# Merging the 16-blocks of eight triangular inverses with 32x32 products on a compact block layout

## The chip, the cores and the metric

The kernel runs on one core of a Trainium2 chip. The metric is the device time of one execution in microseconds. Five engines with an instruction queue each work side by side: TensorE (PE in the rows; its weight loads are PEld), VectorE (DVE), ScalarE (ACT), GpSimd (POOL) and SyncE (SP, which here only starts transfers). An engine takes its instructions in program order; engines wait for each other by semaphores.

## What is computed

Two decoder layers on x of 256 tokens by 1024 features: a gated-DeltaNet layer and a softmax-attention layer, each followed by a residual LayerNorm. The change touches the first layer, where the reference solves a unit lower triangular system in every chunk and head:

```
lower = jnp.where(strict, jnp.einsum('nbhid,nbhjd->nbhij', k_beta, k) * decay, 0.0)
a_mat = jnp.eye(C, dtype=jnp.float32) + lower
w = lax.linalg.triangular_solve(a_mat, k_beta * jnp.exp(gc)[..., None],
                                left_side=True, lower=True, unit_diagonal=True)
u = lax.linalg.triangular_solve(a_mat, v * beta[..., None],
                                left_side=True, lower=True, unit_diagonal=True)
```

## The kernel before

The kernel works with chunks of 128 tokens, so 2 chunks by 8 heads give 16 triangular matrices of 128x128. It inverts them in two groups of four heads, eight matrices (q = 0 to 7) in each. All large products are done as three products of rounded halves (hi times hi, hi times lo, lo times hi); the weights come in units of 128x1024 (`raw`), which ACT rounds (`hi`) and DVE subtracts (`lo`).

The order on TensorE comes out of a planner that runs while the program is built. `Pipeline` holds chains (generators) with a rank; each `yield` says on which engine the next step starts and which tiles it needs, and a step is put out when `Clock`, a model of the engines' times, says that its operands are there. Between chains TensorE gets the next projection products: for the heads' keys and queries (`ps_kq`), values (`ps_v`), gates (`ps_z`, 128x256, six products to two tokens' halves), then the output projection (`ps_y`, 128x512), then the second layer (`ps_bv`, `ps_bkq`, `ps_bz`). The order is fixed once the program is built.

One group's path, in `inverse` (lines 696 to 813):

- The matrices go to memory (`md<-ME`, on POOL's queue) and come back as 64 blocks of 16x16 (`inv<-md`). POOL inverts these by substitution, 15 steps of two small `TENSOR_TENSOR` on `inv`, then a `COPY`, and sends the inverses and their transposes to memory (`td<-inv`). SP brings them back with eight transfers (`TR<-td`) onto the diagonals of `TR`, 128x2x8x128, which POOL has cleared (`MEMSET TR`).
- `merge16` makes 32-blocks out of pairs of 16-blocks with products of full 128x128: M times T (`ps_x`), the result times the transposed inverse (`ps_y`), a masked copy into `TR` on DVE (mask `m32`), and four transposes (`ps_r`) that give the other orientation. It runs twice in a group, on four matrices each.
- `merge32` makes 64-blocks with 32x32 products (`ps_x5`, `ps_y5`; the rows call them `ps_x` and `ps_y`), and the rest of `merges` makes the 128-blocks with 64x64 products (`ps_x6`, `ps_y6`). ACT takes each intermediate out of PSUM into X.
- `solve` (line 860) then multiplies with the values (`ps_s1`, `ps_s2`, `ps_s3`; `ps_s` in the rows), and `read_out` makes the heads' outputs (`ps_o`): squares on ACT, `rs` on DVE and POOL, `og` on DVE, transposes (`ps_og`) on TensorE, and `o` on ACT and DVE, which `ps_y` reads.

The first group's outputs feed the first half of `ps_y` (48 products of 128x512) and the second group's the other 48. After these come the residual and LayerNorm of tokens 0 to 127 (`late`, `x` in the rows; `late` is read from memory into the place of `ME` once the last `ps_o` has read it), whose transposes `ps_t` open the second layer.

## Time and profile before

| | before |
|---|---|
| median of 3 runs | 309.72 us (308.55 to 311.87) |
| the profiled execution, its own time | 308.79 us |
| its span | 307.1 us |
| TensorE busy | 296.2 us, 96% |
| VectorE, ScalarE, GpSimd busy | 204.8, 166.4, 57.5 us |
| granted TensorE clock | 1.00 from 0 to 280 us, 0.94 in the rest |

The span is the time between the first and the last recorded instruction. A matmul's recorded duration goes on after the next one has begun, so what a product costs TensorE is the distance between starts, not its duration; a TensorE that is 96% busy by durations can still be slower or faster per product. A float32 product stands in the records as two, since it takes two passes over its weights.

### The profile page before, as it was taken

To read this page: it belongs to the slowest core of one execution; us is meant where nothing else is said; L and a number is where in the kernel's file an instruction comes from. 1 tells how busy PE (TensorE), PEld (TensorE's weight loads), DVE (VectorE), ACT (ScalarE), POOL (GpSimd) and SP (SyncE) were. 2 spreads that over 40 slices of the span, in tenths; PEclk is the share of its full clock that TensorE was granted. 3 is DMA by queue.
4 is the path that set the end of the run, shared out by engine and by line. 5 is a ranking of instruction groups with operands and counts; after the bars stand their busy time and mean duration, and the time that the engine had idled before them with its cause. 6 is when DMAs were issued, how large, how long until landed. Compare 5 with 4: busy or idle time off the path is not lost. (4 is left out here: it accounts for less than half of the span.)

```text
span 307.1 us, 5956 instructions
## 1 busy us (share of the span) xinstructions
PE 296.2 (96%) x2294; PEld 273.9 (89%) x2294; DVE 204.8 (67%) x440; ACT 166.4 (54%) x341; POOL 57.5 (19%) x114
## 2 busy tenths in 40 slices
PE   8999999999999999999999999999999999999990
PEld 7798988999999999989988678899999999998890
DVE  1589489999996287635475994675655555762645
ACT  3579986557566466655542514875555558461000
POOL 3002310188821886001100110000000000000101
PEclk9999999999999999999999999999999999999997
DMA  6995515565859044504069551896334447400011
GB/s 209 401 288 182 172 45 196 171 228 164 270 128 354 12 143 152 151 3 138 1 213 349 192 205 34 244 339 208 123 130 157 148 152 253 138 2 0 2 68 68
DMA packets 19307, 49.39 MB, mean 161 GB/s; under 512 B 6256, under 2 KB 7152, under 8 KB 19280
## 3 DMA queue, kind: packets, MB, share of 16 engines
q1 hardware_dynamic: 18016, 46.46, 45.4%
q0 software_dynamic: 544, 1.44, 1.8%
q10 hardware_dynamic: 720, 1.11, 1.1%
q8 instruction: 18, 0.29, 0.4%
q14 instruction: 9, 0.07, 0.1%
HBM read 46.65 MB, written 2.36 MB: 160 GB/s over the span
## 5 line engine op out<-in xcount | busy, mean ns | idle before, releaser
L217 DVE TENSOR_TENSOR lo<-raw,hi 128x1024 fp32r<-128x1024 f32 x78 | 94.9, 1226 | 13.1 <-ACT hi L217 12.9
L217 ACT CAST hi<-raw 128x1024 fp32r<-128x1024 f32 x78 | 80.2, 1048 | 16.9 <-PE ps_y L217 8.7
L217 PE MATMUL ps_y<-hi,o 128*128 128x512 f32 (+1 forms) x144 | 41.6, 371 | 0.0
L217 PE MATMUL ps_bkq<-x1h,hi 128*128 128x256 f32 x128 | 38.0, 297 | 0.0
L217 PE MATMUL ps_kq<-xh,hi 128*128 128x256 f32 x128 | 36.8, 288 | 0.0
L217 PE MATMUL ps_kq<-xh,lo 128*128 128x256 f32 x128 | 35.9, 280 | 0.5 <-DVE lo L217 0.5
L217 PE MATMUL ps_kq<-xl,hi 128*128 128x256 f32 x128 | 35.8, 279 | 0.0
L217 PE MATMUL ps_bkq<-x1l,hi 128*128 128x256 f32 x128 | 35.5, 278 | 0.0
L217 PE MATMUL ps_bkq<-x1h,lo 128*128 128x256 f32 x128 | 35.5, 277 | 0.0
L217 POOL TENSOR_TENSOR mv<-mv,nhalf 128x1 f32<-128x1 f32 x4 | 3.8, 949 | 145.9 <-DVE mv L217 145.9
L217 PEld LDWEIGHTS ps_y<-hi,o 128*128 128x128 f32 x144 | 26.1, 188 | 4.6
L217 PE MATMUL ps_y<-lo,o 128*128 128x512 f32 (+1 forms) x72 | 26.4, 367 | 0.0
L217 POOL TENSOR_TENSOR inv<-inv 64x15 f32<-64x15 f32 (+7 forms) x60 | 24.1, 401 | 4.5
L217 PEld LDWEIGHTS ps_kq<-xh,lo 128*128 128x128 f32 x128 | 24.0, 188 | 0.7 <-DVE lo L217 0.7
L217 PEld LDWEIGHTS ps_bkq<-x1h,hi 128*128 128x128 f32 x128 | 24.1, 188 | 0.2
L217 PEld LDWEIGHTS ps_bkq<-x1l,hi 128*128 128x128 f32 x128 | 24.1, 188 | 0.2
L217 PEld LDWEIGHTS ps_kq<-xl,hi 128*128 128x128 f32 x128 | 24.2, 189 | 0.0
L217 PEld LDWEIGHTS ps_kq<-xh,hi 128*128 128x128 f32 x128 | 24.2, 189 | 0.0
L217 DVE SCALAR_TENSOR_TENSOR cv<-ps_kq,cst_sb,cv 128x255 f32<-128x255 f32 (+2 forms) x48 | 21.3, 470 | 4.1 <-ACT cv L217 4.1
L217 PEld LDWEIGHTS ps_bkq<-x1h,lo 128*128 128x128 f32 x128 | 24.0, 188 | 0.0
L217 PE MATMUL ps_v<-xh,hi 128*128 128x256 f32 x64 | 18.6, 291 | 0.0
L217 PE MATMUL ps_bz<-x1h,hi 128*128 128x256 f32 x64 | 18.3, 285 | 0.0
(172 smaller groups left out, 686.7 us busy)
## 6 DMA issues: line engine op xcount, KB each, us to landing
raw<-in_wp_dram SPq DMA_DIRECT2D x78, 512.0 KB, 4.0
md<-ME POOLq DMA_DIRECT2D x8, 128.0 KB, 2.8
late<-in_x_dram SPq DMA_DIRECT2D x1, 1024.0 KB, 7.0
zraw<-in_w_dram ACTq DMA_DIRECT2D x3, 272.0 KB, 5.8
x_sb<-in_xt_dram SPq DMA_DIRECT2D x3, 256.0 KB, 5.6
ag<-in_a_ln_g_dram SPq DMA_DIRECT2D x1, 512.0 KB, 7.7
ab<-in_a_ln_b_dram SPq DMA_DIRECT2D x1, 512.0 KB, 8.4
bg<-in_b_ln_g_dram SPq DMA_DIRECT2D x1, 512.0 KB, 5.8
```

What stands on the lines that cost most here:

```text
L217: r = f(*args, **kw)
```

## The change

The 16-blocks of a group are brought back to a compact layout: of `TR`'s 2048 columns the last part now holds `TC`, 128x2x8x32, where each of the four groups of 32 partitions has its own 32x32 block with two 16-blocks on the diagonal. The eight matrices are handled at once, not four and four.

- The step from 16 to 32 is four 32x32 products per matrix for M times T (`ps_x`, 32 in a group), a masked copy of 128x256 into `XI`, an identity that is set up once per group at the kernel's start, and then eight 32x32 products per matrix (`ps_y`, 64 in a group), which give both orientations: no transposes. ACT copies both into `TC`.
- POOL copies the blocks from `TC` onto the diagonals of `RR` and `T64` (six copies of 32x256 in a group), since the later steps read them there.
- `ps_x5` and `ps_y5` run on `TC` for eight matrices (16 and 24 products), and `ps_x6` and `ps_y6` for eight (8 and 8, as before 4 and 4 twice), with the two halves' roles exchanged.
- The group's steps are one chain that goes on into `solve`. `Clock` charges 15 ns for a product over at most 32 partitions.

```
+                if reads[0].ap[0][1] <= 32:
+                    cost = 15
...
+    XI = [cst.tile([P, 8, 32], F32, name=f"XI{g}") for g in range(2)]
+    for b in blocks:
+        for g in range(2):
+            nc.gpsimd.tensor_copy(XI[g][b], ident[b, b].unsqueeze(1).to_broadcast([32, 8, 32]))
...
-        TR[grp] = act.tile([P, 2, 8, P], F32, tag=f"kq{grp}", name=f"TR{grp}")
-        nc.gpsimd.memset(TR[grp], 0.0)
+        T = act.tile([P, 2048], F32, tag=f"kq{grp}", name=f"TR{grp}")
+        nc.gpsimd.memset(T, 0.0)
+        RR = TR[grp] = T[:, 0:1024].rearrange("p (q c) -> p q c", q=8)
+        TC = T[:, 1024:1536].rearrange("p (w q c) -> p w q c", w=2, q=8)
+        T64 = T[0:64, 1536:2048].rearrange("p (q c) -> p q c", q=8)
...
-        def merge16(q0):
...
-            ps = bank([4, P], "ps_x")
-            for q in range(4):
-                nc.tensor.matmul(ps[:, q, :], ms(q0 + q), TT[:, q0 + q, :], start=True, stop=True)
...
-            for q in range(4):
-                nc.tensor.matmul(ps[:, q, :], RR[:, q0 + q, :], X[:, q, :], start=True, stop=True)
...
-            for q in range(4):
-                nc.tensor.transpose(ps[:, q, :], TT[:, q0 + q, :], ident)
...
-        for q0 in (0, 4):
-            pipe.add(merges(q0), R_INV)
-        pipe.add(solve(grp), R_SOLVE)
+        yield "t", [TC, free("b")]
+        ps = bank([8, 32], "ps_x")
+        for q in range(8):
+            for b in blocks:
+                nc.tensor.matmul(ps[b, q, :], ms(q)[b, b], TC[b, 0, q, :], start=True, stop=True)
+        yield "v", [ps, XI[grp]]
+        nc.vector.copy_predicated(XI[grp], m32.to_broadcast([P, 8, 32]), ps)
+        end(ps)
+        yield "t", [XI[grp], free("b")]
+        ps = bank([2, 8, 32], "ps_y")
+        for q in range(8):
+            for b in blocks:
+                nc.tensor.matmul(ps[b, 0, q, :], TC[b, 1, q, :], XI[grp][b, q, :], start=True, stop=True)
+            for b in blocks:
+                nc.tensor.matmul(ps[b, 1, q, :], XI[grp][b, q, :], TC[b, 1, q, :], start=True, stop=True)
+        yield "a", [ps]
+        nc.scalar.copy(TC, ps)
+        end(ps)
+        yield "t", [TC, free("b")]
+        for b in blocks:
+            nc.gpsimd.tensor_copy(RR[b, :, b], TC[b, 1])
+            if b.start < 64:
+                nc.gpsimd.tensor_copy(T64[b, :, b], TC[b, 0])
...
+        n_inv[grp] = 1
+        yield from solve(grp)
```

The built programs show what the planner makes of it. On POOL, behind the clearing of the second group's tiles (`inv_1311` before, `inv_1323` now), stood its inversion, with the first group's `rs` in its middle:

```order
L217 MEMSET inv_1311 64x16
L217 TENSOR_TENSOR inv_1311<-inv_1311 64x15 x2
...
L217 TENSOR_TENSOR inv_1311<-inv_1311 64x6x10 x2
L217 TENSOR_TENSOR rs<-rs,nhalf 128x4
L217 TENSOR_TENSOR inv_1311<-inv_1311 64x5x11 x2
...
L217 COPY inv_1311<-inv_1311 64x256
L217 DMA td<-inv_1311 64x2x256
```

Now it is:

```order
L219 MEMSET inv_1323 64x16
L219 COPY TR_836<-TR_836 32x8x32 x6
L219 TENSOR_TENSOR inv_1323<-inv_1323 64x15 x2
...
L219 COPY inv_1323<-inv_1323 64x256
L219 TENSOR_TENSOR rs<-rs,nhalf 128x4
L219 DMA td<-inv_1323 64x2x256
```

The first group's six copies stand ahead of the second group's inversion, and `rs` stands between the inversion and its transfer.

On TensorE, where the second group's merges begin (`TR_1314` before, `TR_1326` now), stood:

```order
L217 MATMUL ps_x<-TR_1314,ME 128x128 x8
L217 MATMUL ps_vt<-ident,cv 128x128 x2
L217 MATMUL ps_y<-X,TR_1314 128x128 x8
L217 MATMUL ps_z<-hi_1248,xh 128x256
L217 MATMUL ps_z<-lo_1249,xh 128x256
L217 MATMUL ps_z<-hi_1248,xl 128x256
L217 MATMUL ps_r<-ident,TR_1314 128x128 x4
```

Now it is:

```order
L219 MATMUL ps_x<-TR_1326,ME 32x32 x32
L219 MATMUL ps_og<-ident,og 128x128 x4
L219 MATMUL ps_z<-hi_1298,xh 128x256
...
L219 MATMUL ps_z<-hi_1517,xl 128x256
L219 MATMUL ps_y<-XI_146,TR_1326 32x32 x4
L219 MATMUL ps_y<-TR_1326,XI_146 32x32 x4
```

What moved: between the two groups' first merge products there are now 102 `ps_z` products where there were 57, and the second group's later steps stand between `ps_y` products of the output projection. Before, the second group's first `ps_og` stood ahead of all 96 `ps_y`; now 48 stand ahead of it, and only eight `ps_o` lie between it and the first `ps_y` that reads its result.

At the end of the output projection the second group's last `ps_og` stood 51 `ps_y` products ahead of the first that reads its result. Now these are its rows, `hi_2097` with `lo_2098` being the last weights for tokens 0 to 127, and `hi_1792` the first for tokens 128 to 255:

```order
L219 MATMUL ps_y<-hi_1907,o_2189 128x512
L219 MATMUL ps_og<-ident,og 128x128 x4
L219 MATMUL ps_y<-hi_2097,o_2189 128x512
L219 MATMUL ps_y<-lo_2098,o_2189 128x512
L219 MATMUL ps_y<-hi_2097,o_2189 128x512 x2
L219 MATMUL ps_y<-lo_2098,o_2189 128x512
L219 MATMUL ps_y<-hi_2097,o_2189 128x512
L219 MATMUL ps_y<-hi_1792,o_2189 128x512
```

What moved: six products now stand between the last `ps_og` and the first that reads it.

## Rows read from the trace of the kernel before

**Rows 1.** The page: each engine's busy us, share of the span, instructions.
```profile
PE 296.2 (96%) x2294; PEld 273.9 (89%) x2294; DVE 204.8 (67%) x440; ACT 166.4 (54%) x341; POOL 57.5 (19%) x114
```

**Rows 2.** Waits of TensorE: us in total, times, longest.
```profile
PE ps_t L217 <- DVE x L217: 0.5, 1, 0.5
```

**Rows 3.** Timeline of TensorE: start us, us, what; ends of the first group's merges.
```profile
92.57 1.99 PE L217 MATMUL ps_x<-TR,ME 128*128 128x128 f32 x16
...
104.37 1.05 PE L217 MATMUL ps_s<-W,TR 128*128 128x128 f32 x8
```

**Rows 4.** The same, ends of the second group's merges.
```profile
127.60 1.95 PE L217 MATMUL ps_x<-TR,ME 128*128 128x128 f32 x16
...
139.09 1.05 PE L217 MATMUL ps_s<-W,TR 128*128 128x128 f32 x8
```

**Rows 5.** The same, one 32x32 step between ps_z products.
```profile
99.20 0.28 PE L217 MATMUL ps_z<-hi,xl 128*128 128x256 f32 x1
99.41 0.21 PE L217 MATMUL ps_y<-X,TR 32*32 32x32 f32 x1
99.42 0.22 PE L217 MATMUL ps_y<-TR,X 32*32 32x32 f32 x2
99.47 0.19 PE L217 MATMUL ps_y<-X,TR 32*32 32x32 f32 x1
...
99.66 0.19 PE L217 MATMUL ps_y<-X,TR 32*32 32x32 f32 x1
...
100.01 0.28 PE L217 MATMUL ps_z<-lo,xh 128*128 128x256 f32 x1
```

**Rows 6.** The same, one 64x64 step between ps_z products.
```profile
103.11 0.28 PE L217 MATMUL ps_z<-hi,xl 128*128 128x256 f32 x1
103.31 0.67 PE L217 MATMUL ps_y<-TR,X 64*64 64x64 f32 x8
...
104.14 0.28 PE L217 MATMUL ps_z<-lo,xh 128*128 128x256 f32 x1
```

**Rows 7.** The same, the second group's end and the output projection.
```profile
146.90 0.60 PE L217 MATMUL ps_og<-ident,og 128*128 128x128 f32 x4
...
147.70 1.95 PE L217 MATMUL ps_o<-Z,ME 128*128 128x128 f32 x16
149.40 0.48 PE L217 MATMUL ps_y<-hi,o 128*128 128x512 f32 x1
...
170.99 0.40 PE L217 MATMUL ps_y<-hi,o 128*128 128x512 f32 x1
```

**Rows 8.** Timeline of GpSimd: the last step ahead of the second group's inversion.
```profile
102.90 0.50 POOL L217 MEMSET inv<- 64x256 f32 x2
```

**Rows 9.** GpSimd's instructions by shape: count, busy us, mean ns, idle before.
```profile
L217 POOL TENSOR_TENSOR inv<-inv 64x64 f32<-64x64 f32 x4 | 5.1, 1284 | 0.3
...
L217 POOL COPY inv<-inv 64x256 f32<-64x256 f32 x2 | 1.2, 618 | 0.1
L217 POOL MEMSET inv<- 64x256 f32 x2 | 0.6, 316 | 0.0
```

**Rows 10.** Timeline of SyncE: the second group's last two transfers, the residual's.
```profile
124.48 0.94 SPq L217 DMA_DIRECT2D TR<-td  x2
...
159.55 1.04 SPq L217 DMA_DIRECT2D late<-in_x_dram  x1
```

**Rows 11.** Transfers: count, KB each, median us from issue to landing.
```profile
late<-in_x_dram SPq DMA_DIRECT2D x1, 1024.0 KB, 7.0
...
TR<-td SPq DMA_DIRECT2D x16, 16.0 KB, 2.2
```

**Rows 12.** Timeline of VectorE: long subtractions, an output half, the LayerNorm's start.
```profile
108.03 2.54 DVE L217 TENSOR_TENSOR lo<-raw,hi 128x1024 fp32r<-128x1024 f32 x2
...
148.32 0.75 DVE L217 SCALAR_TENSOR_TENSOR o<-ps_og,nnw,o 128x512 fp32r<-128x512 f32 x1 [1.71 <-ACT o L217]
...
166.63 0.69 DVE L217 SCALAR_TENSOR_TENSOR late<-late,ps_y 128x512 f32<-128x512 f32 x1 [3.20 <-PE ps_y L217]
```

## The prediction

> **What bounds the kernel now.** I read the page first: TensorE is busy for 296.2 of 307.1 us, VectorE for two thirds of it, ScalarE for half [rows 1]. Then the waits of TensorE: there are five kinds with 3.1 us in all, and the only one behind the kernel's first third is 0.5 us on a LayerNorm's output [rows 2]. So in the stretch of the change TensorE has a product to start at almost any moment, and whatever is taken out of its queue shortens the kernel, unless something else then comes too late. I priced the products by the distance of starts in the timeline, since the recorded durations overlap. From the first `ps_y` product of 512 columns at 149.40 to the one at 170.99 [rows 7] there are 92 distances and four transposes, so (21.59 - 0.45)/92 = 0.23 us each; a `ps_z` or `ps_v` product has 256 columns, which I price at half, 0.115 us; and a transpose at 0.11, since from the `ps_og` at 146.90 to the `ps_o` at 147.70 lie four of them and, by the program's order, three `ps_z`: (0.80 - 0.35)/4.

> **What the merges cost now.** The first group's merges stretch from 92.57 to the first `ps_s` at 104.37, 11.80 us [rows 3]. By the program's order 18 `ps_z` products (2.07 us) and four transposes of values (0.44) lie in between, which leaves 9.3 us. The second group's take 11.49 us [rows 4], with 21 `ps_z` and two transposes in them: 8.9 us. Together 18.2 us of TensorE.

> **What they cost after.** One 32x32 step can be priced alone [rows 5]: twelve products, 24 records, between `ps_z` products that start at 99.20 and 100.01. The records come in eight rounds, each with one record of each of three tiles of the array. The rounds from 99.47 to 99.66 are 0.032 us apart (six distances), so eight take 0.26. Of the 0.81 us two `ps_z` take 0.23; the remaining 0.32 is what it costs to go into small tiles and out again. In the new first step four tiles have a product in each round. The three tiles of rows 5 start within 0.01 us of each other and the round waits for its tile to be free again, so I take a fourth as free and price 0.032 us per round too; the other end, each record in its turn, is a rival below.

> Of this the trace shows three tiles that write one PSUM bank side by side: `ps_y5` is one bank, and its records start 0.01 us apart while each lasts 0.2 [rows 5]. [...]

> A group then has: `ps_x`, 16 rounds, 0.51 + 0.32 = 0.83; `ps_y`, 32 rounds, 1.34; `ps_x5` and `ps_y5`, 16 rounds, 0.83 each. A 64x64 step of eight records takes 1.03 - 0.23 = 0.80 with its transitions, and its records are (0.67 - 0.22)/7 = 0.06 us apart (0.22 being one's duration) [rows 6]; sixteen take 1.28, twice. That is 6.4 us a group, 12.8 in all: **5.4 us less** TensorE time, 2.9 of it in the first group.

> **Where TensorE may now wait.** (1) The second group's blocks. Before, the last of SyncE's eight transfers starts at about 124.97 (the second of two in 0.94 us from 124.48) [rows 10] and lands 2.2 us later [rows 11], at 127.2; TensorE begins at 127.60 [rows 4], so 0.4 us of slack. After, two things move. TensorE arrives 2.9 us earlier for the first group's saving, but the planner has put 45 more `ps_z` (5.2 us) and two fewer short transposes (0.2) ahead: 127.6 - 2.9 + 5.2 - 0.2 = 129.7. The blocks come later, since POOL's queue is one line: the first group's six copies stand behind the clearing that ends at 103.40 and ahead of the inversion [rows 8]. `rs` stood inside that stretch and stays in it, so it adds nothing. A copy of 32x256 is not in the trace; by elements per partition it lies between a MEMSET of 256 (0.316 us) and a transposing COPY of 256 (0.618) [rows 9]. I take 0.5, nearer to the copy: 3.0 us. Also, a POOL step that meets a long `lo` subtraction on VectorE stretches: the 64x64 steps have a mean of 1.28 us although a MEMSET of four times the elements takes 0.32 [rows 9], and two of them fell into the 2.54 us of `lo` at 108.03 [rows 12]. Meetings of 0.9 us each are in the inversion now; a stretch that is 3 us longer, with a `lo` every few microseconds, meets about half a one more, 0.5. So the blocks land at 127.2 + 3.5 = 130.7, and TensorE waits **1.0 us**. With copies of 0.32 it waits nothing (127.2 + 1.9 = 129.1); with 0.62 and one more meeting 2.1; if every copy met a `lo`, over 5.

> (2) The first group's copies hold up `ps_x6`, which needs four of them: 103.40 + 2.0 = 105.4. TensorE gets there after `ps_x`, `ps_y`, `ps_x5`, `ps_y5` (3.8), 84 `ps_z` and `ps_v` (9.7) and four transposes (0.4), at 106.5. The cover is 1.1 us; if it is gone each further 0.1 us costs 0.1. Nothing.

> (3) The second group's outputs. From a `ps_og` to its output halves on VectorE it is 146.90 to 148.32 + 0.75 [rows 7, 12], with a semaphore's 0.2 some 2.4 us. Before, dozens of products lay between. Now the first has four transposes and eight `ps_o` behind it, 0.44 + 1.70 (147.70 to 149.40) = 2.1: 0.3 us of waiting. The second has six `ps_y` behind it: 0.44 + 1.37 = 1.8, so 0.6. Together **0.9 us**.

> (4) The first LayerNorm. It starts at 166.63 [rows 12], and the residual, issued at 159.55 [rows 10] with 7.0 us to landing [rows 11], is there at 166.55. It takes the place of `ME`, so it goes out once the last `ps_o` is done. Now from there to tokens 0 to 127 complete there are 24 `ps_y`, one `ps_og` and the waits: 5.5 + 0.4 + 0.6 = 6.5 us, against 7.1 of transfer. The LayerNorm starts up to 0.6 later against TensorE; the wait of rows 2 behind it grows by as much, less the 0.6 that the second wait of (3) gives as cover at the same place: **0.3 us**. If the transfer is held up by weights in SyncE's queue, 1.5.

> Hidden: the masks and the eight copies into `XI` at the start (some 5 us of POOL, which has nothing to do until 27 us); masked copy and PSUM copies on VectorE and ScalarE, which get fewer and smaller, and are busy for 67% and 54%. Were the start not covered, 5 us would be the price.

> **The sum.** -5.4 + 1.0 + 0.9 + 0.3 = -3.2 us. The profiled execution took 308.79 us, its span 307.1 and 1.7 around it; it becomes 305.6. It lies 0.93 below the runs' median of 309.72; the same step from that gives **306.5 us**.

> **Rivals.** A: the forecast, 305.2 to 308.2.

> B: the waits hide. Copies at 0.32 leave the second group's blocks in time, and the covers of (3) and (4) hold but for half a microsecond: 309.7 - 5.4 + 0.5 = 304.8. For it: the planner leaves TensorE almost no wait now [rows 2]. Against: its times know nothing of the stretching by `lo`.

> C: the second group's chain becomes the bound. Copies at 0.62 that meet two `lo` more give 3 us in (1), and a late residual 1.5 in (4) with 0.9 in (3): the gain is eaten, 309.7 - 5.4 + 5.4 = 309.7. For it: slack was 0.4 us already.

> D, slower: the four tiles do not run side by side. A group's 272 records at 32x32 then cost 0.032 each in turn, 8.7 us instead of 2.6, 12.3 more in both; the wait of (1) goes, since TensorE comes 6 us later: 306.5 + 12.3 - 1.0 = 317.8. It decides from a round of 0.052 us on, where 160 rounds eat the 3.2. Against it: three tiles in a round [rows 5]. [...]

> **Numbers.** A 0.47, B 0.25, C 0.21, D 0.06, and 0.01 for a change that does something else. A measurement of this kernel can tell about 1% from no change, that is below 306.6 or above 312.8. Faster takes B and half of A, 0.48; same the other half and nearly all of C, 0.44; slower D and C's end, 0.08. The range of 8 in 10 is 304.0 to 309.7: A and B, and C up to its middle.

> **What would show it.** Right: 32x32 steps whose rounds are 0.03 us apart with four starts each; TensorE 5 us less busy between 92 us and the output projection; a wait of TensorE on a transfer ahead of the second group's `ps_x` of about 1 us; short waits of `ps_y` on `o`. Wrong: rounds of 0.06 us or more (D); POOL copies under 0.35 or over 0.6 us, with the wait gone or 2 us long (B, C); `ps_t` waiting over 1.5 us for `x`. What I can't price from the trace is POOL's copy and how far the residual is from its issue.

## The result, and the profile after

The changed kernel takes 307.22 us (median of 4 runs, 305.22 to 311.05) against 309.36 of the kernel before beside it: 0.989 of its time, 95% interval 0.984 to 0.994. (Ratios here leave out runs more than 1.5% above the fastest of their kernel, as the 311.05.) With 12 runs against 23 (experiment e1) the ratio is 0.995, interval 0.992 to 0.998. So the gain is about 0.5 to 1.1%, 1.7 to 3.3 us; 3.2 were forecast.

From the page of the changed kernel: busy time, the granted clock in 40 slices, and the queue that brings the instructions (packets, MB, share).

```profile
PE 292.2 (95%) x2598; PEld 268.2 (88%) x2598; DVE 201.8 (66%) x432; ACT 162.6 (53%) x327; POOL 67.4 (22%) x137
...
PEclk9999999999999799999999999999999999999996
...
q8 instruction: 20, 0.33, 0.4%
```

TensorE is 4 us less busy than in [rows 1], with 304 records more. The 7 in the row of the clock lies in the first group's merges. The waits of TensorE (us in total, times, longest):

```profile
PE ps_y L219 <- issue: 2.5, 1, 2.5
...
PE ps_t L219 <- DVE x L219: 0.6, 1, 0.6
```

The first row has no counterpart in [rows 2], and no step of the prediction has it. "issue" says that the profile shows nothing that TensorE waited for. The timeline there (start, us, operation, records; idle time before it in brackets):

```profile
96.78 0.21 PE L219 MATMUL ps_y<-TR,XI 32*32 32x32 f32 x4
96.81 0.19 PE L219 MATMUL ps_y<-XI,TR 32*32 32x32 f32 x1
96.81 0.21 PE L219 MATMUL ps_y<-TR,XI 32*32 32x32 f32 x2
99.50 0.23 PE L219 MATMUL ps_y<-XI,TR 32*32 32x32 f32 x4 [2.48 <-issue]
...
99.76 0.44 PE L219 MATMUL ps_vt<-ident,cv 128*128 128x128 f32 x2
99.95 0.44 PE L219 MATMUL ps_z<-hi,xh 128*128 128x256 f32 x1
```

TensorE stops in the middle of one step, between products whose operands are all there, and goes on 2.7 us later. The stop is behind record 227 of the step's 256 (128 weight loads and 128 products), the 1729th of TensorE. By stretches (length in us, busy us of PE, PEld, DVE, ACT and POOL; then granted clock, DMA share, GB/s):

```profile
96.90:99.50 2.60, 0.12 (x15) 0.03 (x2) 0.00 (x0) 0.00 (x0) 1.01 (x2) 1.00 1.01 392
99.50:104.00 4.50, 4.50 (x64) 4.16 (x64) 1.16 (x1) 3.24 (x8) 4.44 (x5) 0.62 0.26 75
```

Behind the stop the granted clock is 0.5 for 3.4 us (100.10 to 103.51), so that the mean of the second stretch is 0.62. In the second group the same steps run without a stop. A product in its turn ahead of each step, the step, and what comes behind:

```profile
133.39 0.28 PE L219 MATMUL ps_z<-hi,xl 128*128 128x256 f32 x1
133.60 0.75 PE L219 MATMUL ps_x<-TR,ME 32*32 32x32 f32 x64
134.28 0.66 PE L219 MATMUL ps_og<-ident,og 128*128 128x128 f32 x4
...
136.00 0.26 PE L219 MATMUL ps_y<-XI,TR 32*32 32x32 f32 x8
...
137.22 0.39 PE L219 MATMUL ps_z<-hi,xh 128*128 128x256 f32 x1
137.45 0.28 PE L219 MATMUL ps_z<-lo,xh 128*128 128x256 f32 x1
...
138.50 0.40 PE L219 MATMUL ps_y<-hi,o 128*128 128x512 f32 x1
138.83 0.69 PE L219 MATMUL ps_x<-TR,ME 32*32 32x32 f32 x32
139.46 0.50 PE L219 MATMUL ps_y<-hi,o 128*128 128x512 f32 x1
139.79 0.39 PE L219 MATMUL ps_y<-lo,o 128*128 128x512 f32 x1
```

`ps_x` takes 64 records in 0.68 us and `ps_y` 128 in 1.22, with four starts per 0.034 us. No wait stands ahead of `ps_x`, where one of 1.0 us was forecast. The group's six steps, with what a product loses behind each (`ps_x5`, the last rows: 139.79 - 138.50 less two products of 0.23 is 0.83), come to 6.5 us.

POOL in the same profile (the first group's copies, the second group's inversion, `rs`, and the write of the blocks):

```profile
103.21 3.14 POOL L219 COPY TR<-TR 32x256 f32<-32x256 f32 x6
106.42 14.04 POOL L219 TENSOR_TENSOR inv<-inv 64x15 f32<-64x15 f32 x30
...
122.28 0.70 POOL L219 DMA_DIRECT2D td<-inv  x1
```

Six copies take 3.14 us, 0.52 each, and 0.5 was forecast; but five of them take 0.39, and one, which lay beside a `lo` for 0.86 us, 1.11. SyncE's transfers of the blocks end their issue at 128.86 instead of 125.42 [rows 10], 3.4 us later, 3.5 forecast; the last lands at 130.54, 130.7 forecast.

So three readings were open: what stops TensorE, what the kernel would be without it, and whether the forecast wait is only hidden by it.

### The profile page after: what moved, and what is told of

Read it like the earlier page. It is cut to its first block, busy times and chain, and to the rows that moved or that the text cites. A ratio compares the mean times of both kernels' runs of the same rounds, so it can differ in the third digit from the quotient of the medians.

```text
span 306.1 us, 6559 instructions
## 1 busy us (share of the span) xinstructions
PE 292.2 (95%) x2598; PEld 268.2 (88%) x2598; DVE 201.8 (66%) x432; ACT 162.6 (53%) x327; POOL 67.4 (22%) x137
## 3 DMA queue, kind: packets, MB, share of 16 engines
q10 hardware_dynamic: 720, 1.11, 1.0%
## 5 line engine op out<-in xcount | busy, mean ns | idle before, releaser
L219 PE MATMUL ps_y<-hi,o 128*128 128x512 f32 (+1 forms) x144 | 43.7, 376 | 0.0
```

Of the source, the lines that this page charges most:

```text
L219: r = f(*args, **kw)
```

## Experiments

**e1, the changed kernel as it is.**

> The changed kernel as it is. [...] Theory F (instruction supply): TensorE's instructions come in pieces of 256 records (a 16 KB transfer of the instruction queue started at 97.34 and took 0.96 us), and ps_y uses a piece up in 1 us. Where the pieces end is fixed by the count of instructions, so the stop comes again behind the same record, 2 to 3.5 us long, and the kernel takes 306 to 308 us. Rival R (a chance event of one execution): no stop, or one elsewhere, and 303 us.

Median 307.13 us, ratio 0.995 (0.992 to 0.998). Its waits:

```profile
PE ps_y L219 <- issue: 2.6, 1, 2.6
...
PE ps_t L219 <- DVE x L219: 1.1, 1, 1.1
```

The stop is again behind record 1729 (counting what the trace has of TensorE: loads, products, semaphores), from 96.67 to 99.48. It is no chance event: F, not R. This time the granted clock stays 1.0 behind it; the execution is one of the two fastest, 305.7 us. Ten of the 12 executions have a mean granted clock of 0.981 to 0.988, as the first profile had; the two with 0.992 and 0.993 are the two fastest.

**e2 and e4, the same instructions at another place in the stream.**

```diff
-WARM = 9
+WARM = 6
...
+    for k in range(41):                       # e4: 60
+        b = slice(32 * (k % 4), 32 * (k % 4) + 32)
+        tc.nc.tensor.matmul(ps_warm[b, 0:32], ones[b, 0:32], ones[b, 0:32], start=True, stop=True)
```

> The changed kernel with three of the nine warming products at the start replaced by 41 small ones of 32x32, so that everything behind stands 152 records later in TensorE's instruction stream; the order of all else is the same. F: the end of a piece now falls 75 records into the first group's ps_y instead of 227, and the piece before it began ahead of ps_x, at about 92.4 instead of 94: the stop comes at about 96.2 and is at most 1.6 us long, or is gone. In the second group the end of a piece moves from 113 records into ps_y to 39 records ahead of it, so the next end falls behind record 217 of it, 2.6 us later: a stop of up to 1 us there that was not there before. Time 1 to 3 us less than the changed kernel. Rival B (the burst of small products, or the place in time with its transfers, stops TensorE whatever the count): the stop stays behind record 227 with 2.5 us, and the second group has none.

> As the shift by 152 records, but with 60 small products: everything stands 228 records later. F: a piece begins with the first record of the first group's ps_y and ends with its last, so TensorE stops at the end of ps_y, behind record 250 to 256, and since the next piece is asked for only as ps_y begins, at 95.9, and came 3.4 us or more after it was asked for, the stop lasts 2.5 to 4.5 us. Time as the changed kernel or up to 2 us more. B: the stop stays behind record 227.

e4: ratio 1.002 (0.998 to 1.006), 0.7% over e1. The first stop moved to the last record of `ps_y`, as F said, and took 3.3 us:

```profile
97.53 0.23 PE L219 MATMUL ps_y<-TR,XI 32*32 32x32 f32 x5
100.89 0.20 PE L219 MATMUL ps_y<-TR,XI 32*32 32x32 f32 x1 [3.14 <-issue]
101.03 0.69 PE L219 MATMUL ps_vt<-ident,cv 128*128 128x128 f32 x2
```

The second group had a stop of 1.6 us too, which I had not listed. Around the end of the first stop and behind it this execution (311.6 us) had a granted clock of 0.5 for 10.2 us. e2: ratio 1.015 (1.010 to 1.019), slower where I expected faster. Its waits:

```profile
PE ps_x L219 <- issue: 3.0, 1, 3.0
PE ps_y L219 <- issue: 1.6, 1, 1.6
```

The second is the one that F put behind record 217 of the second `ps_y`; it is there, 1.8 us long where up to 1 was expected. But the first `ps_y` runs through, and the stop came one piece later, 3.2 us long, in `ps_x5` (the first row). My expectation had only the piece that ends in `ps_y`, not the next, which began there and was used up in 2.8 us. So e2 stops for 5.0 us instead of 2.7, behind either stop the granted clock is 0.5 for 3.4 us, and `ps_x` of the first group waits 0.6 us for its blocks (0.8 in e4).

**f1, a run of small products in the kernel before.** The same loop with `range(160)`, in the old kernel, `WARM` left at 9; one execution.

> The kernel before with 160 products of 32x32 (640 records) behind the nine warming ones at its start, where nothing of the merges stands yet. F (instruction supply): TensorE stops inside the run of small products for 1 to 3 us, and the stop is behind a record whose number from the start is 193 more than a multiple of 256, as the stops so far (1729, 1985, 3009): the first that can be is 449. [...]

```profile
4.92 1.92 PE L487 MATMUL ps_warm<-ones 32*32 32x32 f32 x205
11.09 1.68 PE L487 MATMUL ps_warm<-ones 32*32 32x32 f32 x115 [4.25 <-issue]
```

The timeline shows a stop of 4.4 us behind record 449, the very record, with nothing of the merges near. It is longer than expected. (The run took 319.86 us; TensorE also waits 3.4 us for the first group's blocks there, and I did not take the rest apart.)

Now ends of pieces can be laid side by side. All stops are behind a record 193 more than a multiple of 256; times and transfers (16 KB on the instruction queue) are read from the traces:

| kernel | piece begun | its 256 records done | next record | begun to next | transfer, start to landing |
|---|---|---|---|---|---|
| changed | 94.0 | 96.8 | 99.5 | 5.5 | 97.3 to 98.3 |
| e1 | 93.9 | 96.7 | 99.5 | 5.6 | 97.1 to 98.1 |
| e2 | 95.6 | 98.4 | 101.6 | 6.0 | 98.6 to 100.2 |
| e2, 2nd group | 134.2 | 137.0 | 138.9 | 4.7 | 136.5 to 137.4 |
| e4 | 96.3 | 97.6 | 100.9 | 4.6 | 98.2 to 99.2 |
| e4, 2nd group | 137.3 | 140.2 | 141.8 | 4.5 | 139.4 to 140.4 |
| f1 | 5.6 | 6.7 | 11.1 | 5.5 | 8.5 to 9.5 |
| e3 (below) | 93.5 | 100.1 | 100.1 | 6.6, no stop | 96.8 to 97.8 |
| e3, 2nd group | 133.4 | 138.1 | 138.1 | 4.6, no stop | 135.4 to 136.4 |
| changed, 2nd group | 133.7 | 136.5 | 136.5 | 2.8, no stop | 133.2 to 134.1 |
| f2 (below), 2nd group | 130.9 | 133.8 | 134.0 | 3.0, stop of 0.2 | 131.6 to 132.4 |

In the seven long stops TensorE goes on 4.5 to 6.0 us after it began the piece, and 1.2 to 1.7 us after the transfer has landed. The second is the better rule: in the last two rows a piece is used up in 2.8 us with no stop or hardly one, since the transfer started 0.4 us before, or 0.6 behind, the piece's beginning, and not 2.0 to 3.3 behind it as in the stops. What sets its start no run here tells; that a piece is asked for as the one before it begins, as e4's expectation has it, was an assumption of F. The two longer pieces of e3 in the table (6.6 and 4.6 us) end in no stop, and no piece of the old kernel as it stands ends in one, whose shortest lasts 7.8 us. That the pieces are of 256 records is read off the runs: every stop stands 193 records behind a multiple of 256, the transfers are of 16 KB, and the changed kernel's trace has 20 of them and 20 such places (the old kernel's 18 and 18). How far ahead they are brought no run here shows.

**e3, the first group's `ps_y` held back.**

```diff
-WARM = 9
+WARM, HOLD = 9, 5500
...
-        yield "t", [XI[grp], free("b")]
+        t0 = pipe.now()
+        yield "t", [XI[grp], free("b"), lambda: grp or pipe.now() > t0 + HOLD]
         ps = bank([2, 8, 32], "ps_y")
```

> The changed kernel with the first group's ps_y held back in the planner by about 3.3 us, so that 28 products of ps_z stand between ps_x and it that stood behind it; nothing else of the code differs. F: the piece that is asked for behind ps_x has landed when ps_y needs it, so TensorE does not stop (at most 0.5 us), the granted clock stays 1.0, and 2.7 us of stop and 1.7 us at half clock are saved: ps_x of the second group may then wait for its blocks, up to 2 us, so the kernel takes 302.5 to 305 us, 0.7 to 1.5% under the changed kernel. B (the burst itself stops TensorE): the stop appears again inside ps_y with 2.5 us and the time is that of the changed kernel, 307.

In the trace it is 33 more products of 256 columns (6 `ps_z` and 27 `ps_v`) that stand there, not 28, and `ps_y` starts 3.6 us later than in the changed kernel. Median 305.02 us, ratio 0.987 (0.985 to 0.990): 0.7% under e1, measured beside it, and the lowest ratio here. The waits of TensorE behind the kernel's first third:

```profile
PE ps_t L219 <- DVE x L219: 0.8, 1, 0.8
...
PE ps_vt L219 <- ACT cv L219: 0.3, 1, 0.3
PE ps_y L219 <- issue: 0.2, 1, 0.2
```

The stop is gone but for 0.4 us at the next end of a piece, in `ps_y5` (the last row), and the granted clock stays 1.0. So the stop, with what follows it, costs 0.74% of 309, 2.3 us, where 4.4 (2.7 and 1.7) were expected to be saved. The traces show both parts: the first `ps_t` starts at 167.90 here, at 169.83 in e1 (stop, clock 1.0) and at 170.77 in the changed kernel's profile (stop and half clock). TensorE still does not wait for the second group's blocks. POOL here:

```profile
102.97 2.41 POOL L219 COPY TR<-TR 32x256 f32<-32x256 f32 x6
105.46 12.81 POOL L219 TENSOR_TENSOR inv<-inv 64x15 f32<-64x15 f32 x30
```

The copies take 0.40 us each and the inversion 12.81 instead of 14.04: no copy meets a `lo` subtraction, and the inversion two instead of four. The blocks' issue ends at 126.60, the last lands at 128.28, and TensorE is at `ps_x` at 130.54.

**f2, six more copies on POOL** (with the held `ps_y`, as the runs that follow).

```diff
+        for k in range(0 if grp else 6):
+            tc.nc.gpsimd.tensor_copy(XI[0][blocks[k % 4]], TC[blocks[k % 4], 1])
```

> The kernel with the held ps_y, with six more copies of 32x256 on POOL behind the first group's six, into a tile that nobody reads any more; all else in the same order. In the kernel with the held ps_y the second group's blocks land at about 128.3 to 129.3 (last transfer issued at 126.15, 2.2 to 3.1 us to landing) and TensorE reaches its ps_x at 130.5 without a wait. Theory (POOL's line sets when the blocks land): the blocks come 2.4 to 3.3 us later and TensorE waits 0.5 to 2 us for the transfer, time +0.2 to +1.5 us. Rival (there is more slack than that, or the copies lie beside other work): no wait and the same time within 0.3 us.

Median 306.00, ratio 0.990 (0.984 to 0.995), not to be told from e3. POOL and SyncE's queue:

```profile
104.92 2.65 POOL L773 COPY XI<-TR 32x256 f32<-32x256 f32 x6
```

```profile
124.69 3.77 SPq L219 DMA_DIRECT2D TR<-td  x8
```

The blocks came 1.9 us later (issue ended at 128.46, landing 130.13), and the list of waits has no row for them: `ps_x` starts at 130.88. My theory expected a wait; the rival was right that there was more slack: 2.3 us in e3, 0.7 of it left here.

**f3, the residual loaded early**, into the inversions' buffers (`ag`, `ab`).

> The kernel with the held ps_y, with the residual loaded into the two buffers of the inversions, some 14 us before (ahead of the output projection), and the first LayerNorm's scale and shift put where the residual was. Theory (the residual's transfer sets the first LayerNorm's start): the LayerNorm starts at about 161.5 instead of 162.7, TensorE's wait of 0.8 us of ps_t for x is gone, time 0.6 to 1 us less than with the held ps_y alone. Rival (the sums of ps_y set the start, or the scale and shift now come last): the wait stays, and the time is the same within 0.3 us.

Median 305.70, ratio 0.988 (0.983 to 0.994): no gain to be seen. VectorE's timeline:

```profile
162.81 0.75 DVE L219 SCALAR_TENSOR_TENSOR o<-ps_og,nnw,o 128x512 fp32r<-128x512 f32 x1 [1.74 <-ACT o L219]
163.48 0.68 DVE L219 SCALAR_TENSOR_TENSOR res_ag<-res_ag,ps_y 128x512 f32<-128x512 f32 x1
```

The LayerNorm starts straight behind the last `o` without waiting for a transfer, and the wait of `ps_t` falls from 0.8 to 0.4. But TensorE had lost 0.7 us on an instruction piece in the second group's `ps_y5` (138.54 to 139.26); the residual had been moved while that piece ran (DMA share 0.91 from 134.0 to 138.5). So the residual set the start only by a few tenths. Whether its transfer delayed the instructions is open.

**f4, the planner's price of 15 undone.**

```diff
-                if reads[0].ap[0][1] <= 32:
-                    cost = 15
```

> The kernel with the held ps_y, without the planner's price of 15 for small products, so that it counts 54 for each as before. The order changes in one way that matters: the second group's ps_x stands some 50 products of 256 columns (5.9 us) earlier in TensorE's queue. Theory (the blocks land at 128.3 to 129.3 whatever the planner believes): TensorE reaches ps_x at about 124.5 and waits 3.5 to 4.5 us for the transfer; the products that stood ahead of it come behind and cover waits of the second group, so the kernel is 2.5 to 4.5 us slower than with the price of 15. Rival (the place in the queue does not matter, since the price is only a number): within 0.5 us.

Median 310.66, ratio 1.003 (1.000 to 1.006), 1.6% or 4.9 us over e3. The amount is a little over the expected, and the place is another:

```profile
PE ps_x L217 <- POOL TR L217: 2.2, 1, 2.2
PE ps_vt L217 <- ACT cv L217: 1.6, 2, 1.4
```

The first row is the *first* group's `ps_x6`, which waits for POOL: the planner put the six copies into the middle of the inversion, at 107.60. Behind this wait the granted clock is 0.5 for 6.8 us, from 111.2 on. So an order that the prices make wrong takes back the whole gain. A wait for the second group's blocks never showed: held up before, TensorE came at 129.00 and not at 124.5, and they had landed at 128.13.

**f5, the products in runs of eight for one tile.**

```diff
-        for q in range(8):
-            for b in blocks:
+        for b in blocks:
+            for q in range(8):
```

> The kernel with the held ps_y, with the loops of ps_x and ps_y exchanged: for each block of the partitions all eight matrices, instead of for each matrix all four blocks; the same products, in runs of eight for one tile of the array. The order of all else is the same. Theory of the prediction (a round of 0.033 us is the time until a tile is free again, and the four tiles of a round work side by side): records of one tile in a row come 0.03 us apart each, so ps_y's 128 records take some 4 us instead of 1.1 and ps_x's 64 take 2 instead of 0.6: 4.4 us more in a group, 8.8 in both, less up to 1 us of waits that they hide; time 310 to 315 us. Rival (a record costs its issue, 0.008 us, whatever tile it goes to): the bursts take 1.1 and 0.6 us as now and the time is that of the held kernel, 305.

Median 313.71, ratio 1.0125 (1.003 to 1.022), 2.6% or some 8 us over e3. The timeline:

```profile
93.14 1.91 PE L219 MATMUL ps_x<-TR,ME 32*32 32x32 f32 x64
94.98 0.39 PE L219 MATMUL ps_z<-hi,xh 128*128 128x256 f32 x1
```

`ps_x` takes 1.84 us to the next product instead of 0.68, and `ps_y` 3.46 instead of 1.22: 0.027 us a record against 0.009 (0.032 from start to start within a run of one tile, less where the tile changes). So the round of 0.034 us is about the time of one tile, and four tiles do share it. In steps that is 3.4 us a group, 6.8 in both; 8.8 were expected. Here the granted clock fell to 0.5 for 6.8 us behind the first group's `ps_y`, in which one small tile at a time had worked for 3.4 us, and not behind the second's. So the 8 us are the steps and, in part, the clock: of the four executions the one with a mean clock of 0.996 took 310.9 us, the others, with 0.979 to 0.985, 313.5 to 315.0.

## Why the prediction was right, and where only by luck

**The price of the steps: right.** Before, 18.1 us by the starts of the trace (18.2 in the prediction); after, 6.5 us for a group that is not stopped (6.4). Rounds of 0.034 us with four starts, 0.032 forecast. In each of them four tiles of the array write one PSUM buffer (`ps_x` or `ps_y`) side by side. f5 shows what products in turn would cost, some 7 us in the steps: D is out.

**What was missing: instructions.** The step priced products by their distance and never asked how fast their instructions come. `ps_y` needs 256 instructions in 1.2 us. The stop takes back 2.3 us by the times (2.7 to 2.8 us in the traces, and the clock behind it in most executions).

**(1) The wait for the blocks: mis-sized, +1.0 forecast, 0 measured.** The landing was right in the changed kernel (130.54, 130.7 forecast), in part by luck: a copy alone takes 0.39 us, not 0.5, and one that met a `lo` made up for it. But TensorE came at 133.6, not 129.7, since the stop and the half clock behind it held it up. Without the stop (e3) it comes at 130.5, 0.8 later than forecast, and the blocks are earlier too (128.28), since copies and inversion meet fewer `lo`; f2 used 1.9 us of this room without a wait. Such meetings are what I could not price: 3.14 and 2.41 us for the same six copies.

**(2)** The first group's copies are hidden: no wait ahead of `ps_x6` in the changed kernel. f4 shows what it costs when the cover goes: 2.2 us.

**(3)** Waits on `o`: 0.9 forecast, 0.4 measured; two short ones, 0.25 and 0.16 us of the weight loads, in e3. From `ps_og` to the load it took 2.67 and 2.16 us there, 2.4 forecast; the 0.2 for a semaphore in this was my estimate and too much, since `o` on VectorE starts 0.03 us behind the end of ScalarE's half in the old kernel's trace (147.60 + 0.69 to 148.32), and the loads in e3 start 0.05 us behind the end of `o`:

```profile
156.51 0.30 PEld L219 LDWEIGHTS ps_y<-hi,o 128*128 128x128 f32 x2 [0.25 <-DVE o L219]
162.47 0.30 PEld L219 LDWEIGHTS ps_y<-hi,o 128*128 128x128 f32 x2 [0.16 <-DVE o L219]
```

**(4)** The LayerNorm: 0.3 forecast; `ps_t` waits 0.6, 1.1 and 0.8 us in three profiles against 0.5 [rows 2]. The kind is right, the cause half: f3 leaves 0.4 with the residual out of the way. (That this is the old kernel's only wait behind its first third was misread: `ps_vt` waits 0.4 us at 120.16 there, and 0.3 in e3, which changes nothing in the sum.)

**The sum.** With the stop out (e3): two groups at 6.5 are 5.1 less, 0.4 for `o`, 0.3 for the LayerNorm, 0.4 for the late piece, so -4.0. Measured: span 307.1 to 303.2, -3.9, and by the times -1.3%, 4.0 us. (These two executions are alike in the second layer: 127.4 and 127.5 us from the first `ps_t` to the last product. Others, e1, f2 and f3 among them, have 126.3 to 126.4 there for the same products, so single spans can differ by 1.1 us for a reason that stays open.) With the stop, 2.3 less: -1.7, which is e1's -0.5%. The forecast of -3.2 lies between, because a wait of 1.0 that did not come and 0.5 too much for `o` stood where 2.7 us of stops (2.3 and the late piece's 0.4) and 0.3 of the steps' price were missing. So that the time came out is in part luck, 1.5 us of waits too many against 3.0 us of costs too few; the mechanism was right without its one largest loss. B ("the waits hide") describes e3, not the changed kernel.

## To carry to other kernels

When large products are replaced by many small ones, count instructions per microsecond as well as products: here seven pieces of 256 records that were used up in 1.1 to 2.9 us ended in stops of 1.6 to 4.4 us (not always: one piece of 2.8 us did not), and large products set between the dense steps (33 of them, in e3) were worth 0.7%. Issue small products round robin over the tiles: 0.009 us a record here, against 0.027 in runs for one tile (f5). A saving on the bounding engine makes all that feeds it early or late anew, so price each chain's room, and test it by lengthening it (f2) rather than by the sum alone.
